# A hybrid decoder step on one core: FFN activations in a ring of single chunks, a pool of its own for the conditioning weights, and the mixer's conditioning moved into the first FFN

## The chip, the cores and the metric

The program runs on one core of one Trainium2 chip. The metric is the device time of one execution in microseconds. Names of engines: PE is TensorE (matmuls; PEld are its weight loads), DVE is VectorE, ACT is ScalarE, POOL is GpSimd, SP is SyncE, which here issues nearly all loads from HBM. Lines such as L302 are lines of the kernel before.

## The reference

One layer over 256 prompt tokens and 32 sample tokens (8 sequences of 4), model width 2048, everything in float32:

```
x += 1/2 * g1 * SwiGLU_1(mod(rms(x); sh1, sc1))          # 2048 -> 5632 -> 2048
x += g2 * W_out[ GDN(h) ++ Retention(h) ],  h = mod(rms(x); sh2, sc2)
x += 1/2 * g3 * SwiGLU_2(mod(rms(x); sh3, sc3))
y  = mod(rms(x); shift, scale)
sh1, sc1, g1, ..., sh3, sc3, g3 = split(silu(c) @ w_ada + b_ada, 9)     # per sequence; 2 more for the end
mod(h; shift, scale) = h * (1 + scale) + shift
```

The gated delta rule (GDN) and the retention are chunked recurrences with 8 heads each. The conditioning `silu(c) @ w_ada` has only nine rows (one prompt, eight samples) but a weight of 2048 columns for each of its 11 segments.

## The kernel before

The 288 tokens lie along the free axis and the channels on the partitions. A dense product is cut into weight blocks of 128 output channels. A block of a 2048-deep product (`wg`, `wu`, `win`, `wout`) is 1 MiB and has 16 chunks of 128 x 128, a block of the down product (`wd`) has 11. SP loads a block into a tile of the pool `raw` (4 tiles); ACT copies it to a rounded high part (`whi`, L295) and DVE forms the low part (`wlo`, L298), both in the pool `hilo`, by halves of 8 chunks. Each chunk is then three matmuls into one PSUM tile `acc`: high by high, high by low, low by high (L302 to L304, `three`). The next block is loaded and its first half split while a block runs (`start`, called at chunk 4 of 16 or at once for `wd`).

Conditioning: a segment of 2048 columns takes 16 tiles of 1 MiB (`raw<-wada`, also in the pool `raw`). `ada_tile` (L211) multiplies one tile, as four 32-column matmuls side by side, into the PSUM tile `pada`; after the sixteenth, ACT copies `pada` to `adas`, PE transposes it and DVE adds the bias (`ada_turn`, `ada_out`). A `Feed` is a list of segments. Its `tick(rate)`, called after every weight block, adds to a debt; whenever the debt reaches `BURST`, so many tiles are loaded and multiplied between two blocks. `one` takes a tile at once, `load` issues a load ahead, `until` finishes segments.

Stages in order: the start, where the first norm and the first 16 gate/up chunks run on pieces of the channels as their conditioning (`wadaq`) arrives, with weights `w1q`; the first FFN (to about 968 us); the mixer (to about 1710 us: projections `win`, then `wout`); the second FFN. In an FFN the 44 activation chunks form four groups of `GK` = 11. The gate/up blocks of group g come before the down product of group g - 1, and the activations (`aH`, `aL`: high and low part) of a group are one tile of 11 chunks in a pool with two buffers. Segments 2, 4, 3 are fed from the start through the first FFN, segments 5, 7, 6 in the mixer, segments 8, 10, 9 in the second FFN; a segment must be there before what uses it (4 and 3 for the mixer's norm, 5 for the residual behind `wout`, 7 and 6 for the third norm).

In the mixer each head's small dependent steps (`gdn_task`, `ret_task`, group tasks) are generators; `side.pump`, called after every chunk of a dense product, puts their next step between the chunks, so that on PE a step stands a fixed number of chunks behind the one before. A scheduler then fixes the order of every engine's instructions, moving an instruction back when its inputs are not ready by its own reckoning; on the chip each engine works through its list in order. `decay_rows` (L855) lets POOL load the decay sums of a head into the tile `z` from a small DRAM tensor `gd`, and DVE's subtraction at L861 waits for it.

```
def norm_to_h(nm, A, B, feed):
    feed.one()
    with tc.issue_after(nm.mm.ins):
        feed.one()
    rb, rs = nm.rows(), None
    with tc.issue_after(nm.mm.ins):
        feed.one()
```

These three single tiles stand where PE waits for a norm: before the last sum of squares, after it, and after the row of 1/rms.

Of the kernel before, what the change touches and what calls it, by code (L numbers as in the profile page):

```python
# [9 lines left out]
F32 = mybir.dt.float32  # L10
# [6 lines left out]
P = 128  # L17
# [91 lines left out]
class Side:  # L109
    """Small dependent steps, traced between the chunks of the dense products."""  # L110
# [26 lines left out]
# in slots of one chunk of a dense product: between a side task's steps, after slow steps, between turns  # L137
# [16 lines left out]
def build(tc, a):  # L154
# [27 lines left out]
    cst = cp.tile([P, CW - P], F32, name="cst")  # L182
# [23 lines left out]
    # conditioning: one segment of 2048 columns, 16 row tiles  # L206
# [8 lines left out]
    def ada_turn(ps, n):  # L215
        s = adar.tile([P, 512], F32, name="adas")
# [6 lines left out]
    def ada_out(out, tp, bs, g):  # L223
        """out [P, n, 9] += bias and, for a scale, (1 + .) * gain; tp [P, j, c, 32], block c * j + j"""
# [9 lines left out]
    class Seg:  # L234
# [3 lines left out]
        def step(self, k, w):  # L238
# [48 lines left out]
    # weight tiles, split into two float32r parts  # L287
# [20 lines left out]

    def start(key):
        """load a weight block and split its first half"""  # L310
# [6 lines left out]
    def block_steps(key, xh, xl, pauses=()):  # L317
# [7 lines left out]
        for k in range(nk):  # L325
# [10 lines left out]
            three(ps, hi[:, o:o + P], lo[:, o:o + P], xh[:, k], xl[:, k], k == 0, k == nk - 1)  # L336
# [23 lines left out]
    class Norm:  # L360
        """Sums of squares over the channels, then a row of 1/rms on all partitions."""
# [52 lines left out]
    def sample_post(t, rs, k0, k1, B, eng=None, out=None):  # L414
        """modulated sample columns of some chunks"""
# [4 lines left out]
    def h_chunks(rb, rs, k0, k1, A, B, pre=None):  # L420
        """channel chunks of the modulated norm, split; the first of them as soon as can be"""
# [27 lines left out]
    def norm_to_h(nm, A, B, feed):  # L449
# [4 lines left out]
        with tc.issue_after(nm.mm.ins):  # L454
            feed.one()
# [12 lines left out]
    class Ffn:  # L468
        def __init__(self, wd, gseg, feed, es):
            self.fp = es.enter_context(tc.tile_pool(name="ffn", bufs=2))  # L470
            self.wd, self.gseg, self.feed = wd, gseg, feed

        def acts(self):
            return (self.fp.tile([P, GK, T], F32R, name="aH"), self.fp.tile([P, GK, T], F32R, name="aL"))

        def act(self, pg, pu, aH, aL, i):
# [5 lines left out]
            split(aH[:, i], aL[:, i], t1)  # L482

        def gate_up(self, n, i0, rate, acts=None, skip=0):
            aH, aL = acts or self.acts()
            for i in range(skip, GK):
# [4 lines left out]
                self.act(pg, pu, aH, aL, i)  # L491
            return aH, aL
# [19 lines left out]
    def groups(f, first, n, off, rates, after, aseg, late=None, second=None):  # L512
        """gate/up of a group goes ahead of the down product of the group before"""
        acts = first
        for g in range(1, NG):
            begun = (second, GQ - GK) if g == 1 and second else ()
            nxt = f.gate_up(n, g * GK - off, rates[0] if g == 1 else rates[1], *begun)
# [4 lines left out]
            f.down(g - 1, *acts, rates[2])  # L522
# [1004 lines left out]
```

## Time and profile before

| | |
|---|---|
| three runs | 2621.33, 2621.54, 2629.79 us (median 2621.54) |
| span of the profiled execution | 2625.5 us (the page gives no other time for it) |
| mean granted TensorE clock | 0.992 |
| PE busy with matmuls | 2556.1 us, 97% |
| DVE, ACT, POOL busy | 1548.6, 973.5, 223.2 us |
| moved by DMA | 579.55 MB, 221 GB/s in the mean |

A busy PE in these views is one that has a matmul in flight. The main matmuls start every 0.13 us though each is shown for about 0.30 us, since they overlap; so the time of a piece of PE work is read as the distance between starts. A number in brackets behind a row of the timeline is the idle time of the engine just before it, with what ended it.

### The profile page before, as it was taken

What the parts mean: (1) busy time and instruction counts of PE and PEld (TensorE: products, weight loads), DVE (VectorE), ACT (ScalarE), POOL (GpSimd) and SP (SyncE); (2) the same over time, 40 slices, a digit from 0 to 9 for tenths busy, and PEclk for the clock granted to TensorE, in tenths of its full rate; (3) what the DMA queues carried; (4) which work ended last, traced back from release to release, by engine and by line L of the source; (5) the groups of instructions that cost most, each with busy time, mean ns of one, the idle gap of its engine ahead of it and who ended that gap; (6) DMA issues with size and microseconds to landing.
All of it is one profiled execution on the core that took longest, in us unless ns stands there. A gap on an engine that the chain in (4) does not pass through costs nothing.

```text
span 2625.5 us, 47975 instructions
## 1 busy us (share of the span) xinstructions
PE 2556.1 (97%) x19579; PEld 2383.3 (91%) x19579; DVE 1548.6 (59%) x3435; ACT 973.5 (37%) x1501; POOL 223.2 (9%) x409
## 2 busy tenths in 40 slices
PE   7999999999999999999999999999999999999997
PEld 6888899999999989888888898989999999999997
DVE  4667645445545577666876787664444544554556
ACT  4233433333333345342333333343333333333334
POOL 0000000000000031111311221210000000000002
PEclk9999999999999999999999999999999999999998
DMA  8776766556655685554656656655565655665553
GB/s 313 282 271 250 289 236 235 214 188 219 232 213 184 243 280 200 183 193 160 255 188 239 220 213 248 219 209 213 221 224 188 245 194 210 208 235 198 200 204 114
DMA packets 97357, 579.55 MB, mean 221 GB/s; under 512 B 11431, under 2 KB 11696, under 8 KB 45808
## 3 DMA queue, kind: packets, MB, share of 16 engines
q1 hardware_dynamic: 91472, 558.60, 58.7%
q0 software_dynamic: 5520, 17.82, 2.1%
q8 instruction: 153, 2.51, 0.4%
q14 instruction: 68, 0.56, 0.1%
q10 hardware_dynamic: 144, 0.07, 0.0%
HBM read 561.94 MB, written 14.50 MB: 220 GB/s over the span
## 4 chain that ended last, share of the span: by engine, by line
PE 88%; DVE 5%; DMA 3%; issue 2%; ACT 1%; POOL 1%; ACTq 0%; SPq 0%; POOLq 0%; DVEq 0%
PE acc L302 26%; PE acc L304 26%; PE acc L303 26%; PE pada L211 5%; PE mp L704 3%; DMA raw<-w1q 1%; DMA z<-gd 1%; DVE wlo L298 1%; ACT whi L295 1%; PE mp L1097 0%; DVE hx L426 0%; DVE hL L431 0%; PE mp L833 0%; POOL or L897 0%; DMA xT<-xT 0%
## 5 line engine op out<-in xcount | busy, mean ns | idle before, releaser
L298 DVE TENSOR_TENSOR wlo<-raw,whi 128x512 fp32r<-128x512 f32 (+1 forms) x1408 | 947.9, 701 | 750.8 <-ACT whi L295 739.8
L295 ACT ACTIVATE whi<-raw 128x1024 fp32r<-128x1024 f32 (+1 forms) x768 | 745.6, 971 | 1363.7 <-PE acc L303 998.4
L302 PE MATMUL acc<-hH,whi 128*128 128x288 f32 x4096 | 1237.4, 303 | 13.4 <-POOL hH L441 4.5
L304 PE MATMUL acc<-hH,wlo 128*128 128x288 f32 x4096 | 1216.0, 297 | 0.1
L303 PE MATMUL acc<-hL,whi 128*128 128x288 f32 x4096 | 1201.4, 294 | 0.9 <-DVE hL L444 0.4
L302 PEld LDWEIGHTS acc<-hH,whi 128*128 128x128 f32 x4096 | 773.6, 189 | 79.6 <-issue 35.4
L303 PEld LDWEIGHTS acc<-hL,whi 128*128 128x128 f32 x4096 | 783.4, 191 | 7.9 <-issue 3.8
L304 PEld LDWEIGHTS acc<-hH,wlo 128*128 128x128 f32 x4096 | 770.9, 188 | 1.4 <-DVE wlo L298 0.8
L302 PE MATMUL acc<-aH,whi 128*128 128x288 f32 x1408 | 415.9, 295 | 0.0
L303 PE MATMUL acc<-aL,whi 128*128 128x288 f32 x1408 | 414.8, 295 | 0.0
L304 PE MATMUL acc<-aH,wlo 128*128 128x288 f32 x1408 | 414.4, 294 | 0.0
L302 PEld LDWEIGHTS acc<-aH,whi 128*128 128x128 f32 x1408 | 264.4, 188 | 15.9 <-ACT whi L295 10.9
L304 PEld LDWEIGHTS acc<-aH,wlo 128*128 128x128 f32 x1408 | 264.4, 188 | 0.0
L303 PEld LDWEIGHTS acc<-aL,whi 128*128 128x128 f32 x1408 | 264.3, 188 | 0.0
L211 PE MATMUL pada<-raw,cS 128*32 128x512 f32 (+2 forms) x1792 | 184.4, 519 | 7.6 <-DMA raw<-wadaq 7.6
L211 PEld LDWEIGHTS pada<-raw,cS 128*32 128x32 f32 x1792 | 49.6, 114 | 68.0 <-issue 59.4
L383 POOL TENSOR_TENSOR ss<-ss,hx 128x288 f32<-128x288 f32 x42 | 36.5, 869 | 871.0 <-ACT hx L377 870.3
L462 DVE SCALAR_TENSOR_TENSOR xT<-acc,ada_G,xT 128x256 f32<-128x256 f32 x128 | 61.9, 484 | 22.3 <-PE acc L304 17.7
L481 DVE TENSOR_TENSOR t<-t,acc 128x288 f32<-128x288 f32 x72 | 32.7, 454 | 69.6 <-PE acc L304 69.6
L506 POOL DMA_DIRECT2D xd<-xT x16 | 9.0, 560 | 563.1 <-DVE xT L465 563.1
L355 ACT ACTIVATE aH<-t 128x288 fp32r<-128x288 f32 x88 | 37.8, 429 | 17.4 <-DVE t L481 17.3
L356 DVE TENSOR_TENSOR aL<-t,aH 128x288 fp32r<-128x288 f32 x88 | 39.7, 451 | 0.7 <-ACT aH L355 0.5
(350 smaller groups left out, 1393.1 us busy)
## 6 DMA issues: line engine op xcount, KB each, us to landing
raw<-wada SPq DMA_DIRECT2D x144, 1024.0 KB, 4.8
raw<-wd SPq DMA_DIRECT2D x128, 704.0 KB, 4.2
raw<-wg SPq DMA_DIRECT2D x72, 1024.0 KB, 4.9
raw<-wu SPq DMA_DIRECT2D x72, 1024.0 KB, 5.0
raw<-win SPq DMA_DIRECT2D x64, 1024.0 KB, 4.9
raw<-wadaq SPq DMA_DIRECT2D x32, 1024.0 KB, 6.1
raw<-w1q SPq DMA_DIRECT2D x64, 512.0 KB, 4.4
raw<-wout SPq DMA_DIRECT2D x16, 1024.0 KB, 5.7
```

Of the source, the lines that this page charges most:

```text
L211: mm = E.matmul(ps[32 * c:32 * c + 32, :n], cS[:, k, :], w[:, n * c:n * c + n], start=(k == 0), stop=(k == NC - 1), skip_group_check=True, ...
L295: S.activation(hi[:, b], src[:, b], AF.Copy)
L298: V.tensor_tensor(lo[:, b], src[:, b], hi[:, b].bitcast(F32), ALU.subtract)
L302: E.matmul(ps[:, :T], h_, xh, start=first, stop=False)
L303: E.matmul(ps[:, :T], h_, xl, start=False, stop=False)
L304: E.matmul(ps[:, :T], l_, xh, start=False, stop=last)
L355: S.activation(hi, x, AF.Copy)
L356: V.tensor_tensor(lo, x, hi.bitcast(F32), ALU.subtract)
L383: G.tensor_tensor(self.ss, self.ss, sq, ALU.add)
L462: V.scalar_tensor_tensor(xT[:, j, :SEQ], ps[:, :SEQ], g[:, j, 0:1], x0[:, :SEQ], ALU.mult, ALU.add)
L481: V.tensor_tensor(t1, t1, pu[:, :T], ALU.mult)
L704: E.matmul(out, lhsT, rhs, start=start, stop=stop, skip_group_check=True)
```

## The change

- The activations are single chunks in a ring of `GK + LEAD` = 20 tiles each for `aH` and `aL`, where they were two tiles of 11 (and, at the start, further ones for partial sums). With that, the gate/up blocks of a group are split: 9 of its 11 chunks go before the down product of the group before, 2 after it.
- Conditioning weights get a pool of their own (`adaw`, 3 tiles) in both FFNs; `raw` is left to the weight blocks there. In the mixer the two tiles that are still loaded ahead lie in `raw`.
- `BURST` is 3 where it was 2. Each `tick` issues one load ahead when fewer than three are under way.
- Segments 5, 7, 6 join the first feed, with higher rates; the `feed.tick` and `feed.until` calls in the mixer are gone. In the first `norm_to_h` three tiles (of segment 8) stand behind the row of 1/rms, where it was one.
- The table `cst` moves from the permanent pool to the mixer's pool and is loaded at the mixer's beginning, by POOL; `adas` shares a tag with `wlo`; the outputs of the conditioning have two buffers each.

```diff
-BURST = 2
+BURST = 3
+LEAD = 9
...
-    cst = cp.tile([P, CW - P], F32, name="cst")
...
-        s = adar.tile([P, 512], F32, name="adas")
+        s = hilo.tile([P, 512], F32, name="adas", tag="wlo")
...
-                out = res[self.seg] = adar.tile([P, NC, 9], F32, name=t, tag=t)
+                out = res[self.seg] = adar.tile([P, NC, 9], F32, name=t, tag=t, bufs=2)
...
+            self.pool = raw
...
-                w = raw.tile([P, D], F32, name="raw")
+                w = self.pool.tile([P, D], F32, name="raw")
...
         def tick(self, rate):
             self.debt += rate
+            if len(self.ahead) < BURST:
+                self.load()
             while self.debt >= BURST:
...
-    def norm_to_h(nm, A, B, feed):
+    def norm_to_h(nm, A, B, feed, more):
...
-            feed.one()
+            for _ in range(more):
+                feed.one()
...
+            feed.pool = es.enter_context(tc.tile_pool(name="adaw", bufs=BURST))
...
-        def acts(self):
-            return (self.fp.tile([P, GK, T], F32R, name="aH"), self.fp.tile([P, GK, T], F32R, name="aL"))
+        def slot(self, name, dt=F32R):
+            return self.fp.tile([P, T], dt, name=name, tag=name[:2], bufs=GK + LEAD)
...
-            split(aH[:, i], aL[:, i], t1)
+            aH.append(self.slot("aH"))
+            aL.append(self.slot("aL"))
+            split(aH[-1], aL[-1], t1)
...
-            nxt = f.gate_up(n, g * GK - off, rates[0] if g == 1 else rates[1], *begun)
+            f.gate_up(n, g * GK - off, rates[0], LEAD, *nxt)
...
-            f.down(g - 1, *acts, rates[2])
+            f.down(g - 1, *acts, rates[1])
+            f.gate_up(n, g * GK - off, rates[0], GK, *nxt)
...
-    feed = Feed([(2, "GQ"), (4, "A", 1), (3, "B")])
+    feed = Feed([(2, "GQ"), (4, "A", 1), (3, "B"), (5, "G"), (7, "A", 2), (6, "B")])
...
-            w = raw.tile([P, D], F32, name="raw")
+            w = feed.pool.tile([P, D], F32, name="raw")
             nc.sync.dma_start(out=w, in_=a["wadaq"][PIECE0[self.n] + self.i])
...
-    feed = Feed([(5, "G"), (7, "A", 2), (6, "B")])
-    nm = groups(ff, acts[0], 1, GQ, (0.45, 0.3, 0.32), feed, 4, late, acts[1])
+    feed2 = Feed([(8, "GQ"), (10, "A", 3), (9, "B")])
+    feed2.pool = feed.pool
+    nm = groups(ff, acts[0], 1, GQ, (0.87, 0.6), feed2, 4, 6, late, acts[1])
+    norm_to_h(nm, res[4], res[3], feed2, 3)
     fs.close()
-    norm_to_h(nm, res[4], res[3], feed)
-    feed2 = Feed([(8, "GQ"), (10, "A", 3), (9, "B")])
+    feed2.pool = raw
     nm = mixer(tc, a, locals())
...
-    first = ff.gate_up(2, 0, 0.4)
-    nm = groups(ff, first, 2, 0, (0.4, 0.3, 0.32), None, 10)
+    ff.gate_up(2, 0, 0.35, GK, *first)
+    nm = groups(ff, first, 2, 0, (0.35, 0.32), None, 10, 3)
...
-    cst = L["cst"]
+    cst = c1.tile([P, CW - P], F32, name="cst")
+    nc.gpsimd.dma_start(out=cst, in_=a["cst"][:, P:])
...
             ps = block("win", 8 * i + h)
-            feed.tick(RATE)
...
-    feed.until(1)
...
-LOADS = (14, 15)
+LOADS = (13, 14, 15)
```

How the order of instructions moves is shown at three places. On SP, at the mixer's beginning, the loads of the kernel before alternate between `win` blocks, conditioning tiles (`wada`) and states of the recurrence (`st<-sg`), and go on with three `win` and two `wada` in turn through the whole mixer:

```order
L314 DMA raw<-win 128x2048
L262 DMA raw<-wada 128x2048
L1078 DMA st_11964<-sg 128x1024
L314 DMA raw<-win 128x2048 x3
L262 DMA raw<-wada 128x2048
L1078 DMA st_11997<-sg 128x1024
L1078 DMA st_12043<-sg 128x1024
L1078 DMA st_12104<-sg 128x1024
L262 DMA raw<-wada 128x2048
L314 DMA raw<-win 128x2048 x3
```

The same place on SP after the change:

```order
L266 DMA raw<-wada 128x2048 x3
L323 DMA raw<-win 128x2048 x3
L266 DMA raw<-wada 128x2048 x2
L323 DMA raw<-win 128x2048
L1085 DMA st_12367<-sg 128x1024
L1085 DMA st_12400<-sg 128x1024
L1085 DMA st_12446<-sg 128x1024
L1085 DMA st_12507<-sg 128x1024
L323 DMA raw<-win 128x2048 x31
```

Five conditioning tiles are loaded around the mixer's beginning, and then none until its last blocks: 31 `win` loads stand in a row.

On PE, also in the mixer, a burst of two tiles (`pada`) stood between two blocks of the kernel before; three chunks of the second block follow, and then a head's transposes (`fv`, L1004):

```order
L304 MATMUL acc_12347<-hH_84,wlo_12349 128x288
L211 MATMUL pada_10294<-raw_12430,cS_94 32x512 x4
L211 MATMUL pada_10294<-raw_12436,cS_94 32x512 x4
L302 MATMUL acc_12459<-hH_84,whi_12376 128x288
L303 MATMUL acc_12459<-hL_85,whi_12376 128x288
```

The same blocks on PE after the change (here `acc_12738` and `acc_12838`), with the transposes again three chunks into the second:

```order
L309 MATMUL acc_12738<-hL_85,whi_12739 128x288
L310 MATMUL acc_12738<-hH_84,wlo_12740 128x288
L308 MATMUL acc_12838<-hH_84,whi_12767 128x288
L309 MATMUL acc_12838<-hL_85,whi_12767 128x288
L310 MATMUL acc_12838<-hH_84,wlo_12768 128x288
```

The burst is gone and the transposes stand behind the same chunks as before, so PE comes to them earlier by the burst.

On SP, at a down product of the first FFN, the kernel before has pairs of conditioning loads between six or seven `wd` loads:

```order
L314 DMA raw<-wu 128x2048
L262 DMA raw<-wada 128x2048 x2
L314 DMA raw<-wd 128x1408 x7
L262 DMA raw<-wada 128x2048 x2
L314 DMA raw<-wd 128x1408 x6
```

After the change, at a down product of the first FFN:

```order
L323 DMA raw<-wu 128x2048
L323 DMA raw<-wd 128x1408
L266 DMA raw<-wada 128x2048 x3
L323 DMA raw<-wd 128x1408 x4
L266 DMA raw<-wada 128x2048 x3
```

Three conditioning loads now stand in a row between four `wd` loads.

## Rows read from the trace of the kernel before

**Rows 1.** The page's first part: engine, busy us, share of the span, instructions.
```profile
PE 2556.1 (97%) x19579; PEld 2383.3 (91%) x19579; DVE 1548.6 (59%) x3435; ACT 973.5 (37%) x1501; POOL 223.2 (9%) x409
```

**Rows 2.** Windows: stretch, length, busy of PE, PEld, DVE, ACT, POOL; clock, DMA share, GB/s.
```profile
10.00:20.00 10.00, 5.12 (x78) 4.82 (x82) 4.95 (x14) 3.70 (x11) 0.87 (x1) 1.00 1.01 422
300.00:968.00 668.00, 667.91 (x5063) 637.29 (x5062) 353.12 (x697) 242.17 (x312) 22.69 (x36) 1.00 0.62 222
990.00:1640.00 650.00, 628.06 (x4782) 566.06 (x4781) 468.77 (x1278) 246.72 (x524) 137.16 (x253) 0.99 0.58 209
```

**Rows 3.** PE's timeline around a burst of two tiles: start, us, engine, line, names.
```profile
1991.09 0.29 PE L304 MATMUL acc<-hH,wlo 128*128 128x288 f32 x1
1991.31 1.92 PE L211 MATMUL pada<-raw,cS 128*32 128x512 f32 x16
1993.17 0.40 PE L302 MATMUL acc<-hH,whi 128*128 128x288 f32 x1
```

**Rows 4.** PE's timeline around a single tile.
```profile
2536.84 0.29 PE L304 MATMUL acc<-aH,wlo 128*128 128x288 f32 x1
2537.07 1.06 PE L211 MATMUL pada<-raw,cS 128*32 128x512 f32 x8
2538.06 0.40 PE L302 MATMUL acc<-aH,whi 128*128 128x288 f32 x1
```

**Rows 5.** Windows of pada's instructions alone: PE, PEld, ACT, clock, DMA share, GB/s.
```profile
977.00:1640.00 663.00, 48.17 (x360) 9.53 (x360) 1.80 (x3) 0.99 0.58 212
```

**Rows 6.** PE's timeline at the mixer's norm.
```profile
973.58 1.07 PE L211 MATMUL pada<-raw,cS 128*32 128x512 f32 x8
976.28 0.29 PE L721 MATMUL acc<-hH,whi 128*32 128x288 f32 x1 [1.64 <-DVE hs L418]
```

**Rows 7.** PE's waits from 20 to 300 us: total, times, longest.
```profile
PE acc L302 <- ACT whi L295: 1.7, 3, 1.1
...
PE pada L211 <- DMA raw<-wadaq: 1.3, 2, 0.7
```

**Rows 8.** The chain of waits from 262 to 282 us: start, us, what.
```profile
263.77 3.24 DMA raw<-w1q
...
268.42 8.23 DMA raw<-w1q
```

**Rows 9.** PE's timeline in the mixer: two bursts and the waits behind them.
```profile
1143.98 1.92 PE L211 MATMUL pada<-raw,cS 128*32 128x512 f32 x16
...
1151.15 0.48 PE L1004 MATMUL mp<-ident,fv 128*128 128x128 f32 x1 [2.51 <-DVE bv L1005]
...
1385.17 1.93 PE L211 MATMUL pada<-raw,cS 128*32 128x512 f32 x16
...
1394.52 0.30 PE L989 MATMUL mp<-ident,fq 128*128 128x128 f32 x1 [2.99 <-DVE fq L941]
```

**Rows 10.** PE's waits from 990 to 1650 us: total, times, longest.
```profile
PE mp L704 <- ACT vn L1034: 3.0, 2, 1.6
```

**Rows 11.** DVE's waits from 1000 to 1640 us: total, times, longest.
```profile
DVE d L861 <- DMA z<-gd: 20.7, 6, 4.8
```

**Rows 12.** The tile z: its DMAs' time to landing.
```profile
DMA to landing us min/median/max: 3.4/6.2/7.6
```

**Rows 13.** DMA issues from 1383 to 1392 us: KB each, median us to landing.
```profile
raw<-win SPq DMA_DIRECT2D x2, 1024.0 KB, 9.1
raw<-wada SPq DMA_DIRECT2D x1, 1024.0 KB, 12.1
...
z<-gd POOLq DMA_DIRECT2D x1, 128.0 KB, 7.6
```

**Rows 14.** Window behind the wait at 1148 us; columns as in Rows 2.
```profile
1151.00:1154.40 3.40, 3.25 (x15) 3.23 (x15) 1.95 (x8) 1.39 (x3) 0.28 (x2) 0.50 0.88 371
```

**Rows 15.** DMA issues of the whole span: KB each, median us to landing.
```profile
raw<-wada SPq DMA_DIRECT2D x144, 1024.0 KB, 4.8
...
cst<-cst POOLq DMA_DIRECT2D x1, 1211.0 KB, 8.4
```

More of the change, by code (lines that the diff above doesn't have):

```diff
@@ L307, in build, with chunk @@
     pre = {}
+    def chunk(x, k):
+        return x[k] if isinstance(x, list) else x[:, k]
     def start(key):
@@ L335, in block_steps @@
             o = k % 8 * P
-            three(ps, hi[:, o:o + P], lo[:, o:o + P], xh[:, k], xl[:, k], k == 0, k == nk - 1)
+            three(ps, hi[:, o:o + P], lo[:, o:o + P], chunk(xh, k), chunk(xl, k), k == 0, k == nk - 1)
         return ps
@@ L481, in act, with gate_up @@
             V.tensor_tensor(t1, t1, pu[:, :T], ALU.mult)
-            split(aH[:, i], aL[:, i], t1)
-        def gate_up(self, n, i0, rate, acts=None, skip=0):
-            aH, aL = acts or self.acts()
-            for i in range(skip, GK):
+            aH.append(self.slot("aH"))
+            aL.append(self.slot("aL"))
+            split(aH[-1], aL[-1], t1)
+        def gate_up(self, n, i0, rate, i1, aH, aL):
+            for i in range(len(aH), i1):
                 pg = block(f"wg{n}", i0 + i)
@@ L510, in down, with groups @@
                         nm.later.append(put)
-    def groups(f, first, n, off, rates, after, aseg, late=None, second=None):
-        acts = first
+    def groups(f, acts, n, off, rates, after, aseg, nseg, late=None, second=None):
         for g in range(1, NG):
-            begun = (second, GQ - GK) if g == 1 and second else ()
-            nxt = f.gate_up(n, g * GK - off, rates[0] if g == 1 else rates[1], *begun)
+            nxt = second if g == 1 and second else ([], [])
+            f.gate_up(n, g * GK - off, rates[0], LEAD, *nxt)
             if g == 1:
@@ L521, in groups @@
                     late()
-            f.down(g - 1, *acts, rates[2])
+            f.down(g - 1, *acts, rates[1])
+            f.gate_up(n, g * GK - off, rates[0], GK, *nxt)
             acts = nxt
         nm = Norm()
-        f.down(NG - 1, *acts, rates[2], nm, after, aseg, off > 0)
-        f.feed.until(3)
+        f.down(NG - 1, *acts, rates[1], nm, after, aseg, off > 0)
+        f.feed.until(nseg)
         return nm
     fs = ExitStack()
-    feed = Feed([(2, "GQ"), (4, "A", 1), (3, "B")])
+    feed = Feed([(2, "GQ"), (4, "A", 1), (3, "B"), (5, "G"), (7, "A", 2), (6, "B")])
     ff = Ffn("wd1", 2, feed, fs)
-    A1 = adar.tile([P, NC, 9], F32, name="ada_A", tag="ada_A")
-    B1 = adar.tile([P, NC, 9], F32, name="ada_B", tag="ada_B")
+    A1 = adar.tile([P, NC, 9], F32, name="ada_A", tag="ada_A", bufs=2)
+    B1 = adar.tile([P, NC, 9], F32, name="ada_B", tag="ada_B", bufs=2)
     class Piece:
@@ L586, in build @@
     rB = ff.fp.tile([P, T], F32, name="rB", bufs=1)
-    part = [(ff.fp.tile([P, GK, T], F32, name=n), ff.fp.tile([P, GQ - GK, T], F32, name=f"{n}q", bufs=1))
-            for n in ("aH", "aL")]
-    part = [[x[:, i] for x, n in ((t, GK), (u, GQ - GK)) for i in range(n)] for t, u in part]
+    part = [[ff.slot(n, F32) for _ in range(GQ)] for n in ("aHq", "aLq")]
     off = 0
-    acts = []
+    acts = [([], []), ([], [])]
     for n, (k0, k1) in enumerate(PIECES):
@@ L617, in build @@
                 if last:
-                    if i in (0, GK):
-                        acts.append(ff.acts())
-                    ff.act(part[0][i], part[1][i], *acts[i // GK], i % GK)
+                    ff.act(part[0][i], part[1][i], *acts[i // GK])
             if not last:
@@ L675, in mixer @@
     pv, bc, mp, acc, xT, hH, hL = (L[k] for k in ("pv", "bc", "mp", "acc", "xT", "hH", "hL"))
-    ident, ones1, mhalf, feed, res = (L[k] for k in ("ident", "ones1", "mhalf", "feed", "res"))
+    ident, ones1, mhalf, res = (L[k] for k in ("ident", "ones1", "mhalf", "res"))
     block, split, residual, side, b4 = (L[k] for k in ("block", "split", "residual", "side", "b4"))
@@ L976, in gdn_head @@
         ps = block("win", 24 + h)
-        feed.tick(RATE)
         gate(ps, f["z"], gt["z"][:, cs])
@@ L1412, in ffn @@
     def ffn(n, g0, off):
-        gu = lambda g: [(f"w{w}{n}", i, NC) for i in range(max(0, g * GK - off), (g + 1) * GK - off) for w in "gu"]
+        gu = lambda g, i0, i1: [(f"w{w}{n}", i, NC) for i in range(max(0, g * GK - off + i0), g * GK - off + i1) for w in "gu"]
         dn = lambda g: [(f"wd{n}", g * NC + j, GK) for j in range(NC)]
-        r = gu(0) if g0 == 0 else []
+        r = gu(0, 0, GK) if g0 == 0 else []
         for g in range(1, NG):
-            r += gu(g) + dn(g - 1)
+            r += gu(g, 0, LEAD) + dn(g - 1) + gu(g, LEAD, GK)
         return r + dn(NG - 1)
```

22 lines of the change are left out of this document (6 added, 16 removed).

## Prediction

> **What bounds the kernel now.** I read the page's first part, then busy time by stage, then PE's and DVE's waits where PE is not full, then the timeline around single bursts. PE has a matmul in flight for 2556.1 of 2625.5 us [rows 1]. In the first FFN it lacks 0.1 us of 668 (667.91), while DMA moves 222 GB/s; the reader is to see that nothing there waits for a load. In the mixer it lacks 21.9 us of 650 (650 - 628.06) [rows 2]. So a change gains where it takes work from PE or shortens the mixer's waits; a load that comes earlier in an FFN gains nothing. The profiled span is 2625.5 us; the runs lie at 2621.33 to 2629.79 with a median of 2621.54. I make the sum against the span and take it off the median.
>
> **Longer bursts.** A burst of two tiles puts 1993.17 - 1991.09 = 2.08 us between two starts of PE that are otherwise 0.13 apart: 1.95 us [rows 3]. A single tile makes 2538.06 - 2536.84 = 1.22, so 1.09 us [rows 4]. A further tile thus costs 0.86 us and the visit itself 0.23 us. Three tiles, which no row shows, should cost 1.95 + 0.86 = 2.81; the bounds are 1.95 + 1.09 (nothing saved) and 1.95 + 0.73 (another 0.13 saved). The order of instructions has 86 visits for the 144 `wada` tiles before and 64 after: 22 x 0.23 = 5.1 us off, with bounds 0 and 8. The tiles themselves are as many as before.
>
> **Two more tiles at the mixer's norm.** PE idles 1.64 us there after its third single tile [rows 6]. The change puts five tiles in place of three. But its fourth and fifth need the places of the first two, so their loads start late, and in PE's order they stand behind 12 and 29 matmuls of the next product, whose chunks of h arrive no faster than DVE makes them. They fill part of that slack: two tiles that elsewhere cost 2 x 0.86 are worth between 0 and 1.7 us, and I take 1.0 off.
>
> **The start.** From 20 to 300 us PE waits 1.3 us for `wadaq` and 1.7 us for ACT's `whi` [rows 7]; behind the latter stand loads of `w1q` that take 3.24 and 8.23 us of the chain, just after a burst [rows 8], because bursts and weights share four tiles. With three tiles more both have their places ahead. The waits can go wholly (3.0 off) or stay; the stretch from 10 to 20 us, where DMA is full (share 1.01) [rows 2], does not change. I take 2.0 off.
>
> **The mixer's conditioning goes to the first FFN.** 45 tiles (360 records of 8 to a tile) leave the mixer [rows 5], about 22 visits of 1.95 us = 43 us, and cost the same in the first FFN, where PE has no idle time to hide them. What decides is how much of the 43 us PE really gains in the mixer. There the bursts stood between a product and the side steps that wait for DVE or ACT, and gave these time. Two places show it: 7.2 us after a burst starts PE waits 2.51 us for the transposes of `fv`, and 9.4 us after another it waits 2.99 us for `fq` [rows 9]. With the burst gone, PE comes to them earlier and waits 1.95 us longer unless DVE is quicker too. Two waits for ACT's `vn`, 3.0 us together [rows 10], follow a burst as closely. Four such places: 4 x 1.95 = 7.8 us on. Steps that now arrive just in time would add to this; all 22 visits would be 43 us.
>
> Against it: DVE works in order, and in this stretch it stands 20.7 us in six waits for the DMA of `z` [rows 11], which lands after 3.4 to 7.6 us, in the median 6.2 [rows 12]. In the case behind the 2.99 us, two `win` blocks and a conditioning tile were issued within the same few us and took 9.1 and 12.1 us, and `z` 7.6 [rows 13]. After the change the mixer loads only `win`, one block as each of four places comes free, so `z` should land nearer its 3.4. If half of the 2.8 us between median and minimum comes off at four places, that is 4 x 1.4 = 5.6 off. The Trainium skill, DMA: Bandwidth & Descriptors, Issuing engines are not separate DMA queues, says that loads of all issuing engines run on the same 16 DMA engines and interleave; rows 13 agree (7.6 us beside full queues, against 3.4 at best), and by that rule alone most of the 2.8 us would come off, which is the rival on the faster side below. I take 7.8 - 5.6 = 2 us on for the mixer; its bounds are 17 off (all but 5 of the 21.9 us) and 43 on.
>
> **Edits at nothing.** Three conditioning loads in a row ahead of a weight block in the first FFN: the stage moved 222 GB/s x 668 us = 148 MB; with 48 more tiles (50 MB) in 668 + 45 us it needs 278 GB/s, and 422 were reached from 10 to 20 us [rows 2]. The cover is the ring of four `raw` tiles, now for weights alone; without it see the rival. The split gate/up: chunk 10's activation is read 30 matmuls (3.9 us) into the first down block, and only the last group lacks other blocks between; 0, at most 1 us at each of two places. `cst` is issued by POOL before the norm's power and lands after 8.4 us [rows 15]; its first reader stands 88 matmuls (11.6 us) behind the norm; 0, at most 2. `adas` takes a place of `wlo` once a segment, so that DVE's next split starts up to four chunks later and still ends within the block; 0, at most 0.5 us in 9 segments.
>
> **Sum.** -5.1 - 1.0 - 2.0 + 2 = -6.1 us: 2619.4 on the span, 2615.4 on the median. Forecast 2615.5 us, with 2606 to 2626 as its own range.
>
> **Rivals.**
>
> *z lands at its best (faster).* If every `z` takes 3.4 us, DVE's 20.7 us shrink to 20.7 - 6 x 2.8 = 3.9, and the PE waits that hang on it go in spite of the lost cover: about 15 of the 21.9 us, and with them a stretch of half clock. After the 2.51 us wait the granted clock was 0.50 for 3.4 us [rows 14], which is 1.2 in place of 2.4 GHz and costs 1.7 us. That gives -8.1 - 15 - 1.7 = -25: 2597 us. For it: the crowded queue at just these places. Against it: 18 of the 22 bursts had no named wait behind them that a faster `z` could remove, and the best of nine landings need not become the rule.
>
> *The lost cover comes back as waits (slower).* PE in the mixer reaches its side steps 1.95 us early at most of the 22 places, and DVE, busy 468.77 of 650 us [rows 2] and soon of some 607, does not follow. It decides the sign from 22 / 1.95 = 11 places on (8.1 + 13 us to be more than 0.5% slower); at 13 places it is 25 us: 2621.5 - 8.1 + 25 = 2638. For it: side steps follow each other by fixed numbers of chunks. Against it: only four places wait now, and the scheduler has put the transposes of `fq` 14 to 20 matmuls further back where the burst went. The Trainium skill, TensorE: Matmul & The Clock Gate, The HAM clock gate, says that the array's clock falls to half after idling; rows 14 agree (0.50 after a 2.51 us wait), and by it every second such wait would cost 1.7 us more.
>
> *Weights come late in the first FFN (slower).* Two `win` blocks issued together took 9.1 us, 4.55 each [rows 13]; at that pace three tiles and a `wd` block take 13.7 + 3.1 = 16.8 us, and three `wd` blocks of PE work only 3 x 33 x 0.132 = 13.1. 3.7 us at each of 64 x 0.6 / 3 = 13 visits is 47; half of it gives 2639 us. For it: SP's order has the three in a row. Against it: a single tile landed in 4.8 us with others beside it [rows 15], pairs with fewer free places cost no wait in the stage before, and 422 GB/s needs 9 us for the same bytes.
>
> *The order does not do what it says:* the third tile's load waits for a place and splits the bursts. Then the visits stay at 86 and -5.1 falls away: 2620.5 us, no change. A place comes free 25 us before it is needed, so I give it little.
>
> **Chances.** Forecast 0.53, z at its best 0.22, lost cover 0.12, late weights 0.08, split bursts 0.05. A change of 0.5%, 13 us, is about what a measurement of this kernel can tell from none; faster than that means below 2608.4, slower above 2634.6. Faster: 0.22 and 0.05 of the forecast's own spread, 0.27. Slower: 0.11 of lost cover and 0.05 of late weights, together 0.16. The same: 0.57. The range 2596 to 2638 leaves out the half of the fast rival beyond its centre and most of the slow cases' upper part, 0.2 together.
>
> **What would show it.** Right: visits of three tiles with 2.94 us between the neighbouring starts; PE still full from 300 us to the end of the first FFN, which ends some 43 us later, and a mixer shorter by about 41; `z` landing in 4 to 5 us; no `w1q` in the chain at 260 to 290 us. Wrong: a mixer shorter by under 25 us (lost cover) or by over 50 (z); PE waiting for `whi` or `wlo` in the first FFN, with `wd` loads that land after 10 us and more.

## The result and the profile after

The changed kernel takes 2604.47 us in the median (2602.56 to 2604.69), the kernel before 2623.78 beside it: ratio 0.9916, 95% interval 0.9901 to 0.9931. The forecast of 2615.5 had the sign and a third of the size. The result lies inside the prediction's range of 2596 to 2638, but below the forecast's own (2606 to 2626), on the faster side, to which the prediction gave 0.27. A repeat gave 2602.98 against 2627.86, ratio 0.9904 [0.9890, 0.9919]. The profiled spans are 2625.5 and 2602.6 us, 22.9 apart. A span is 1.8 us shorter than the measured time of the same execution (2604.39 us for the one profiled after, 0.1 below its median); by this the execution profiled before took about 2627.3 us (an estimate, its time is not on record), 3.5 above its median, so some 3.6 us of the 22.9 are this execution's.

The page's first part after the change, where PE's busy time falls by 13.7 us against [rows 1]:

```profile
PE 2542.4 (98%) x19579; PEld 2378.5 (91%) x19579; DVE 1541.1 (59%) x3435; ACT 974.0 (37%) x1501; POOL 217.7 (8%) x408
```

The first FFN and the mixer of [rows 2] after the change, moved to where they now lie (columns as there):

```profile
300.00:1004.00 704.00, 704.00 (x5362) 640.77 (x5361) 348.47 (x701) 238.76 (x310) 22.31 (x34) 1.00 0.73 275
1026.00:1640.00 614.00, 593.25 (x4539) 568.45 (x4538) 476.04 (x1290) 251.97 (x531) 137.29 (x262) 1.00 0.43 154
```

The first FFN carries 275 GB/s and PE lacks nothing of 704 us; the mixer carries 154 and PE still lacks 20.75 us (614.00 - 593.25), where it lacked 21.9. So the transfers moved and PE's idle time stayed.

Whole stages show the rest. They begin with the first dense matmul of the start, of the first FFN, of the mixer and of the second FFN. The mixer's window alone begins later, behind the matmuls that stand among the pieces of its norm: 6.2 us after the first FFN's end before, 8.8 after the change, which now hold two conditioning tiles. Before:

```profile
24.60:229.00 204.40, 195.51 (x1679) 171.61 (x1679) 118.38 (x241) 71.24 (x99) 8.35 (x19) 0.98 0.78 279
229.00:976.30 747.30, 743.25 (x5615) 701.70 (x5616) 415.32 (x837) 276.64 (x368) 27.83 (x47) 1.00 0.64 228
982.50:1716.40 733.90, 709.58 (x5390) 643.11 (x5388) 526.16 (x1388) 279.83 (x569) 158.58 (x288) 1.00 0.58 210
1716.40:2608.40 892.00, 889.39 (x6708) 850.93 (x6709) 466.58 (x907) 326.51 (x422) 17.96 (x27) 1.00 0.57 206
```

After:

```profile
24.50:221.60 197.10, 192.53 (x1689) 169.34 (x1689) 118.34 (x239) 71.16 (x99) 8.73 (x19) 0.99 0.83 296
221.60:1012.60 791.00, 788.59 (x6000) 714.69 (x6001) 415.60 (x852) 279.25 (x371) 27.91 (x46) 1.00 0.74 279
1021.40:1700.60 679.20, 656.23 (x5017) 628.35 (x5016) 516.67 (x1369) 275.89 (x562) 152.60 (x288) 1.00 0.45 158
1700.60:2585.40 884.80, 883.98 (x6667) 850.64 (x6668) 465.70 (x907) 327.05 (x422) 17.94 (x27) 1.00 0.56 202
```

Length less busy is PE's idle time: 8.9, 4.1, 24.3 and 2.6 us before, 4.6, 2.4, 23.0 and 0.8 after. That is 9.1 us less, 4.3 of it at the start. Over the whole span it is 69.4 and 60.2 us, 9.2 less, so the parts that these windows leave out have no share in it.

The granted clock is the second source. Before, it stood at 0.50 or 0.51 in these stretches (1.2 in place of 2.4 GHz):

```profile
24.60:28.00 3.40, 3.37 (x25) 2.65 (x26) 2.45 (x6) 1.06 (x1) 0.00 (x0) 0.50 0.78 261
99.70:106.50 6.80, 5.07 (x20) 4.98 (x21) 6.14 (x12) 3.82 (x6) 1.97 (x5) 0.50 0.83 288
229.40:232.80 3.40, 3.40 (x16) 3.27 (x15) 2.85 (x6) 0.51 (x1) 0.18 (x1) 0.50 0.36 147
976.90:980.30 3.40, 3.23 (x14) 2.75 (x15) 3.40 (x10) 1.42 (x3) 3.18 (x9) 0.50 1.02 419
1219.20:1222.60 3.40, 3.40 (x16) 1.98 (x16) 2.19 (x7) 0.00 (x0) 0.84 (x2) 0.51 0.27 34
1717.60:1721.00 3.40, 3.28 (x14) 2.96 (x14) 3.40 (x10) 1.85 (x5) 2.64 (x6) 0.50 1.01 424
```

With [rows 14] that is 27.2 us. The program's last 13.6 us before and 14.7 after are at half clock as well; PE does next to nothing there (1.49 us in both), and they are left out. After the change there are two stretches:

```profile
24.50:27.90 3.40, 3.38 (x25) 2.66 (x26) 2.87 (x7) 1.06 (x1) 0.00 (x0) 0.50 1.03 414
1014.40:1017.80 3.40, 3.40 (x16) 1.33 (x16) 3.40 (x9) 1.97 (x6) 2.11 (x5) 0.50 1.00 419
```

In the repeat the first of them was absent and its start took 195.70 us in place of 197.10, with the same instructions and the same idle time (4.6 us): by this pair of executions one such stretch costs 1.4 us. The other stood behind the norm again.

```profile
24.00:219.70 195.70, 191.12 (x1690) 168.22 (x1690) 118.42 (x239) 71.30 (x99) 8.73 (x19) 1.00 0.83 300
```

Third, the visits. A visit is an unbroken run of conditioning matmuls on PE. From the first dense matmul on the conditioning has 117 visits before and 93 after (parts of a burst that a side step cuts count apart). A burst of three answers to [rows 3]:

```profile
611.20 0.29 PE L310 MATMUL acc<-aH,wlo 128*128 128x288 f32 x1
611.42 2.78 PE L212 MATMUL pada<-raw,cS 128*32 128x512 f32 x24
614.14 0.40 PE L308 MATMUL acc<-aH,whi 128*128 128x288 f32 x1
```

614.14 - 611.20 = 2.94 us, as forecast. Together: idle -9.1, clock -(27.2 - 6.8) / 3.4 x 1.4 = -8.4, visits -24 x 0.23 = -5.5, in all -23.0 of the 22.9 seen. The idle time and the number of visits are read; the price of a visit is that of whole bursts, and the clock's part is the price of one stretch times six. PE's busy time fell by 13.7, and clock and visits make 13.9 of it.

DVE's wait for `z` in 1034 to 1650 us, against [rows 11], and its landing, against [rows 12]:

```profile
DVE d L870 <- DMA z<-gd: 10.3, 4, 3.2
```
```profile
DMA to landing us min/median/max: 3.4/4.8/8.1
```

Half of DVE's wait is gone. PE's idle time in the mixer hardly moved, yet it was cut differently: the waits of 2.51 and 2.99 us of [rows 9] are gone, and the longest named one is 1.9 us. PE's waits from 1026 to 1700 us:

```profile
PE mp L1076 <- DVE on L907: 5.9, 6, 1.7
PE mp L831 <- DVE Tn L1032: 2.9, 5, 0.7
PE mp L1350 <- DVE on L920: 2.3, 2, 1.2
PE mp L1319 <- DVE on L920: 1.9, 1, 1.9
PE mp L1011 <- DVE bv L1012: 1.3, 3, 0.4
```

### The profile page after: what moved, and what is told of

Same layout as the page of the kernel before. It is cut to its first block, busy times and chain, and to the rows that moved or that the text cites. A ratio compares the mean times of both kernels' runs of the same rounds, so it can differ in the third digit from the quotient of the medians.

```text
span 2602.6 us, 47978 instructions
## 1 busy us (share of the span) xinstructions
PE 2542.4 (98%) x19579; PEld 2378.5 (91%) x19579; DVE 1541.1 (59%) x3435; ACT 974.0 (37%) x1501; POOL 217.7 (8%) x408
## 3 DMA queue, kind: packets, MB, share of 16 engines
q8 instruction: 153, 2.51, 0.4%
## 4 chain that ended last, share of the span: by engine, by line
PE 90%; DVE 5%; POOL 2%; issue 1%; ACT 1%; DMA 1%; SPq 0%; ACTq 0%; POOLq 0%; DVEq 0%
PE acc L308 27%; PE acc L309 26%; PE acc L310 26%; PE pada L212 6%; PE mp L713 2%; DVE wlo L304 1%; PE mp L1104 0%; DMA z<-gd 0%; PE mp L842 0%; POOL rv L918 0%; ACT whi L301 0%; POOL or L906 0%; ACT kd L882 0%; ACT y L673 0%; DMA xT<-xT 0%
## 5 line engine op out<-in xcount | busy, mean ns | idle before, releaser
L308 PE MATMUL acc<-hH,whi 128*128 128x288 f32 x4096 | 1222.2, 299 | 8.3 <-POOL hH L450 4.0
L309 PEld LDWEIGHTS acc<-hL,whi 128*128 128x128 f32 x4096 | 771.0, 188 | 6.4 <-issue 2.1
L308 PEld LDWEIGHTS acc<-aH,whi 128*128 128x128 f32 x1408 | 263.9, 187 | 16.8 <-issue 15.9
L212 PE MATMUL pada<-raw,cS 128*32 128x512 f32 (+2 forms) x1792 | 178.8, 520 | 6.5 <-DMA raw<-wadaq 6.4
L627 DVE TENSOR_TENSOR aLq<-acc,aLq 128x288 f32<-128x288 f32 x64 | 29.1, 455 | 26.6 <-PE acc L310 26.2
```

The costliest lines, as they stand in the source:

```text
L212: mm = E.matmul(ps[32 * c:32 * c + 32, :n], cS[:, k, :], w[:, n * c:n * c + n], start=(k == 0), stop=(k == NC - 1), skip_group_check=True, ...
L308: E.matmul(ps[:, :T], h_, xh, start=first, stop=False)
L309: E.matmul(ps[:, :T], h_, xl, start=False, stop=False)
L627: V.tensor_tensor(dst, ps[:, :T], dst, ALU.add)
```

## The experiments

Ratios are to the kernel before, run on the same chip in the same rounds; intervals are 95%. The changed kernel's own is 0.9916, and 0.9904 in the repeat. A profile shows one execution, and its span is compared with the 2602.6 us of the changed kernel's.

**Bursts of two in the changed kernel.**

```diff
-BURST = 3
+BURST = 2
...
-            feed.pool = es.enter_context(tc.tile_pool(name="adaw", bufs=BURST))
+            feed.pool = es.enter_context(tc.tile_pool(name="adaw", bufs=3))
```

> The changed kernel with bursts of two tiles in place of three; the pool of three tiles stays. If a visit of PE to the conditioning costs 0.23 us whatever its length, 22 more visits cost 5.1 us: 2609.6 us against the changed kernel's 2604.5, and 2.08 us between the starts around each pair. If a longer burst saves nothing (each tile 0.98 us), 2604.5. If the loads of three in a row cost waits in the first FFN, it is faster: below 2602.

Measured 2611.55 us, 0.9947 [0.9933, 0.9961]; span 2607.9, 5.3 above the changed kernel's. There are 107 visits in place of 93, 14 more and not the 22 expected: 14 x 0.23 = 3.2. A further 1.8 us is idle time in the first FFN (one wait of 3.4 us for a `wada` tile; with `BURST` at 2, `tick` also keeps only two loads ahead, though the pool has three places). Together that is 5.0 of the 5.3, so the price of a visit holds. By the medians the difference is 7.1 us; the profiled execution is 1.8 us faster than its median.

**The mixer's conditioning back in the mixer,** in twos through `raw`. The rates of the FFNs follow, and one tile stands behind the row of 1/rms of the mixer's norm; all else is as changed.

```diff
-    feed = Feed([(2, "GQ"), (4, "A", 1), (3, "B"), (5, "G"), (7, "A", 2), (6, "B")])
+    feed = Feed([(2, "GQ"), (4, "A", 1), (3, "B")])
...
+    feed1 = Feed([(5, "G"), (7, "A", 2), (6, "B")])
+    feed1.burst = 2
...
+            L["feed1"].tick(RATE)
```

> The changed kernel with segments 5, 7 and 6 given back to the mixer, in pairs through the pool raw as in the kernel before; ring, own pool in the FFNs, bursts of three there and the start stay. Theory (the move gains by the granted clock and little else): the mixer's idle time of PE stays at 23 to 25 us, some half-clock stretches come back in it, and some 9 more visits cost 2 us: 2604.5 + 2 + 3.4 + 1 = 2611 us. Rival one (z lands late again and PE waits for it): idle time of the mixer 30 us and more, 2616 or above. Rival two (the move only lost cover): PE's idle time in the mixer falls by 8 us and more and the kernel is faster than 2602.

Measured 2613.16 us, 0.9949 [0.9935, 0.9963]; span 2610.3. Two rows of PE's timeline in the mixer, each with the wait ahead of it:

```profile
1138.82 0.48 PE L1016 MATMUL mp<-ident,fv 128*128 128x128 f32 x1 [2.48 <-DVE bv L1017]
```
```profile
1380.31 0.30 PE L1001 MATMUL mp<-ident,fq 128*128 128x128 f32 x1 [3.38 <-DVE fq L953]
```

The two long waits are back, and at each the clock fell (columns as in [rows 2]):

```profile
1138.20:1141.60 3.40, 2.78 (x12) 2.77 (x13) 2.42 (x9) 1.38 (x4) 0.28 (x2) 0.50 0.99 417
1380.50:1383.90 3.40, 3.40 (x18) 3.40 (x17) 2.71 (x9) 2.77 (x14) 0.72 (x3) 0.51 0.94 389
```

Idle time in the mixer is 24.0 us against 23.0. By this run, 7.7 us longer in its span, the move is worth its visits (108 against 93, 3.5 us) and the mixer's clock (6.8 us of half clock against none, 2.8), little else. This agrees with both the forecast (two effects that cancel) and a theory that neither exists; the two runs with one side cut, below, tell them apart.

**The move alone,** made to the kernel before, with the second buffers for the conditioning's outputs and the place of `adas` that go with it.

```diff
-    feed = Feed([(2, "GQ"), (4, "A", 1), (3, "B")])
+    feed = Feed([(2, "GQ"), (4, "A", 1), (3, "B"), (5, "G"), (7, "A", 2), (6, "B")])
...
-    nm = groups(ff, acts[0], 1, GQ, (0.45, 0.3, 0.32), feed, 4, late, acts[1])
+    nm = groups(ff, acts[0], 1, GQ, (0.9, 0.68, 0.68), feed2, 4, late, acts[1])
...
-            feed.tick(RATE)
```

> The kernel before, with one part of the change alone: the segments 5, 7 and 6 are multiplied in FFN1, at twice its rate of conditioning, and the mixer holds none; tiles still come in twos through the shared pool, and the activations keep their ring. Theory (the move saves switches into the conditioning's matmuls only where bursts grow, and half clock in the mixer; TensorE's waits in the mixer do not come from the conditioning): switches stay at about 115, so nothing there; half clock in the mixer 6.8 us to 0, worth 3.4; idle time of the mixer stays at 23 to 25 us; about 2621 against the before of the same chip (ratio 0.998), down to 2616 if a stretch of half clock goes at the start by chance. Rival, loads out of the mixer are worth its z waits: 2626 - 10 = 2616 with idle at 14 to 18 us. Rival, lost cover: idle at 30 us or more and no gain. Rival, FFN1's shared pool can't feed twice the rate: FFN1's idle time rises from 4 to over 10 us.

Measured 2639.34 us, 1.0063 [1.0050, 1.0077]: 0.6% slower. The mixer does as expected (idle 24.0, no half clock); the visits are 107, not the 115 expected. The first FFN's waits decide. The longest of PE's from 300 to 1750 us:

```profile
PE pada L211 <- DMA raw<-wada: 10.0, 5, 4.8
```

The two long ones, 8.8 us together, stand at 1018 to 1033 us, where the last two tiles of the six segments are loaded only as they are multiplied, and beside them the clock stood at half for 17.1 us. The first FFN took 815.0 us, against 798.2 in the changed kernel with twos: 9.5 us more idle and 14.9 us more at half clock (6.1 us at 1.4 a stretch, 7.5 if half of the time is lost) make nearly all of these 16.8. The rival of the shared pool has its sign, 13.7 us of idle time in the first FFN against 4.1 before. In this form, with these rates, the move costs more than it brings. In the changed kernel these tiles are loaded ahead into a pool of their own; that this, and not a higher rate, is what makes the move pay is argued and not shown.

**The start's loads back in `raw`,** in the changed kernel.

```diff
-            w = feed.pool.tile([P, D], F32, name="raw")
+            w = raw.tile([P, D], F32, name="raw")
```

> The changed kernel with the start's conditioning tiles (wadaq) back in the pool raw, which they then share with the start's weights as in the kernel before; all else stays. Theory (the start's 7 us come from the own pool: waits of 3 us for loads, and the half-clock stretch of 6.8 us at 100 us that they bring on): the 1152nd main matmul starts at 229 us again and not at 221.6, 2612 us. Rival (the start gained by its order or by chance of the clock): 2604.5 us, with the stretch at 100 us still away.

Measured 2612.16 us, 0.9942 [0.9928, 0.9957]. Its start, with one stretch of half clock as in the profile after:

```profile
24.80:227.00 202.20, 193.94 (x1689) 169.30 (x1689) 116.83 (x239) 71.78 (x99) 8.57 (x19) 0.99 0.82 289
```

202.20 against 197.10: by this profile the pool is worth 5.1 us at the start, 3.7 of it idle time (8.3 against 4.6). The stretch of half clock at 100 us did not come back in it. But the profiled execution (2608.22 us, granted clock 0.997) is the fastest of five; the other four have 0.994 or 0.995 and up to 2613.50 us, and the median is 7.7 us above the changed kernel's. What these lost, and whether that stretch is part of it, no profile shows.

**The mixer's cover cut, its loads kept,** in the kernel before. Here cover means the time that a burst gives the other engines before PE's next side step; the kernel leaves out most of the product that fills it.

```diff
-            ada_tile(self.ps, k, w, 512)
+            ada_tile(self.ps, k, w, 16 if sliver and k else 512)
```

> The kernel before, with the mixer's conditioning loads and bursts kept, but each conditioning matmul of the mixer behind a segment's first tile covers 16 columns in place of 512 (most of that product is left out). So the transfers of the mixer stay, and nearly all of the work that could cover TensorE's waits goes: 45 tiles of about 0.98 us less some 0.2 that remain, 35 us. Theory (waits of the mixer are not covered by the conditioning): idle time of TensorE in the mixer stays at 24 us, VectorE's waits for z at about 20 us, the mixer falls from 734 to about 699, in all about 2590. Rival, lost cover: idle rises by 8 us or more to over 32, in all about 2598 or above. Rival, the transfers set the waits: with the bursts shorter the loads press the z transfers more and idle rises together with the z waits.

Measured 2599.35 us, 0.9900 [0.9887, 0.9914].

**The mixer's loads cut, its cover kept,** in the kernel before.

```diff
-            if s < len(self.q):
+            if s < len(self.q) and self.still:
+                self.ahead.append(hH.rearrange("p k t -> p (k t)")[:, :D].bitcast(F32))
+            elif s < len(self.q):
```

> The kernel before, with the mixer's conditioning bursts kept on TensorE but fed from a resident tile, so that their 48 loads of 1 MB are left out (these segments hold wrong values). The complement of the kernel with short matmuls: cover stays, transfers go. Theory (the z transfers are waited for by VectorE and not passed on to TensorE): VectorE's waits for z fall from 20 to about 10 us, idle time of TensorE in the mixer stays at 23 to 25 us, the mixer at 730 to 734, about 2624 (ratio 0.9985 to 1.0). Rival, faster z transfers are worth what VectorE no longer waits for: idle 14 to 18, the mixer at 724 to 728, about 2617.

Measured 2622.74 us, 0.9982 [0.9972, 0.9991]. The kernel leaves out 45 loads (99 of `wada` in place of 144), since the norm's three stand ahead of the mixer. The mixer with the cover cut, and below it with the loads cut:

```profile
981.10:1686.90 705.80, 676.19 (x5389) 639.32 (x5387) 519.37 (x1389) 278.90 (x568) 153.16 (x288) 1.00 0.60 219
```
```profile
979.40:1705.70 726.30, 707.96 (x5383) 642.08 (x5382) 525.19 (x1385) 278.78 (x566) 158.74 (x288) 1.00 0.42 147
```

Idle time is 29.6 us with the cover cut and 18.3 with the loads cut, against 24.3: 5.3 up and 6.0 down. Profiles that differ only outside the mixer have 22.9 to 24.6 there, so both are more than their spread. DVE's waits for `z`, 1000 to 1640 us, in the one and the other, against [rows 11]:

```profile
DVE d L865 <- DMA z<-gd: 16.9, 5, 4.7
```
```profile
DVE d L865 <- DMA z<-gd: 14.4, 6, 3.1
```

The rival by which shorter bursts let the loads press `z` harder falls: with the cover cut the waits for `z` are shorter, not longer. The theory of these two runs, that neither effect exists, fell by the idle time, which is one profile each: the bursts did cover waits, and the loads did make some. The time of the second run alone would not tell. Its median is only 3.8 us below the 2626.51 of the kernel before, near the theory's 2624, and the profiled execution (2616.42) is the fastest of eleven. The granted clock goes with this spread: it is 0.995 in the five executions of up to 2619.97 us and 0.993 or 0.994 in the six from 2622.74 on.

**One tile, not three, behind the row of 1/rms at the mixer's norm.**

```diff
-    norm_to_h(nm, res[4], res[3], feed2, 3)
+    norm_to_h(nm, res[4], res[3], feed2, 1)
```

> The changed kernel with one tile in place of three behind the row of the mixer's norm. Theory: the two tiles fill slack of PE that is there anyway and cost 2 x 0.86 us where they go instead: 2604.5 + 1 to 1.7 = 2606 us. Rival: they only push the mixer's first products back by their own length: 2604.5, no change. The half-clock stretch behind the norm stays in both.

Measured 2605.8 us, 0.9922 [0.9907, 0.9937]; span 2603.2, 0.6 above. That profile had one more stretch of half clock (at 1698.9 us, 1.4 us); without it, it would be 0.8 us faster than the changed kernel's. By the medians it is 1.3 us slower, as the theory has it. Even the sign is open: inconclusive.

**Bursts of four, five chunks ahead.**

```diff
-BURST = 3
+BURST = 4
...
-LEAD = 9
+LEAD = 5
```

> The changed kernel with bursts of four tiles and loads held five ahead in place of three tiles and nine ahead. Theory (each switch into and out of the conditioning's matmuls costs 0.23 us, bursts hold nothing up): switches fall from 93 to about 78, so 3.5 us less, about 2603 against 2606 for the changed kernel on this chip (ratio 0.991). Rival, longer bursts hold up the engines that wait for FFN1's tiles: FFN1's idle time rises from 2.4 to 6 us or more, and nothing is gained. Rival, five ahead is too few beside bursts of four: TensorE waits for a conditioning weight at some bursts, 2 to 4 us each, 2610 or more.

Measured 2606.9 us, 0.9928 [0.9914, 0.9941]. There are 74 visits, but in the first FFN PE waits for tiles:

```profile
PE pada L212 <- DMA raw<-wada: 6.4, 5, 2.1
```

From 288 us on, among these waits, 10.2 us are at half clock. There `f.feed.until(1)` stands behind the first `LEAD` chunks; with five, the first segment is not yet done and its last tiles are multiplied as they land.

**Bursts of four, seven chunks ahead** (`LEAD = 7`), and the changed kernel again beside it.

> The changed kernel with bursts of four tiles and seven activation chunks ahead of a down product in place of three and nine. Theory (each visit costs 0.23 us; what the kernel with four tiles and five chunks ahead lost, 5.5 us of idle time and 10.2 us of half clock, came at one place, where the first segment had to be finished after ten blocks and its last tiles were multiplied as they landed; with seven ahead 12 of its 16 tiles are done by then and the other 4 are loaded): visits about 75 against 93, FFN1's idle time back at 2 to 3 us and no half clock in it, 4 us less than the changed kernel: about 2600 (ratio 0.990 to this chip's before). Rival, four loads in a row press the weights behind them: FFN1's idle time stays at 6 us or more, 2605 or above.

> The changed kernel itself, on the same chip and in the same rounds as the kernel with bursts of four and seven ahead, for a direct comparison: 2604 to 2606 (ratio 0.9916 to this chip's before). What its profile shows again is taken as its own: visits 93, idle time of the mixer 22 to 25 us, no half clock in the mixer. Theory that half clock outside the mixer falls by chance: its stretches at the start or behind the norm stand elsewhere than in the first profile. Rival, they are a fixed property: the same two, at 24 and 1014 us.

Measured 2599.42 us (2598.55 to 2600.08), 0.9890 [0.9873, 0.9906], against 2602.98 (2602.17 to 2603.67) on the same chip: 3.6 us less, and the two ranges do not meet. Its burst of four:

```profile
656.51 0.29 PE L310 MATMUL acc<-hH,wlo 128*128 128x288 f32 x1
656.74 3.64 PE L212 MATMUL pada<-raw,cS 128*32 128x512 f32 x32
660.31 0.40 PE L308 MATMUL acc<-hH,whi 128*128 128x288 f32 x1
```

3.80 us between starts is 2.94 + 0.86 again. There are 74 visits, 19 fewer than 93: -4.4 us. The first FFN idles 3.6 us, 1.2 more than in the changed kernel and above the 2 to 3 expected; 2.8 of them are one wait for a tile at the norm, at the place where the changed kernel waits 1.63 us for DVE. -4.4 + 1.2 is -3.2 of the -3.6. This version beats both kernels.

## Why the prediction was right in sign and small in size

The span fell by 22.9 us where the forecast had 6.1. The 16.8 us between them are, nearly, 8.4 of the clock, 4.0 of the start, 3.3 of the mixer's idle time, 1.8 of the second FFN's and 0.4 of the visits, less the 1.0 forecast for the norm.

**Longer bursts (-5.1): the price right, the number partly by luck.** The trace has 2.94 us for three tiles, 3.80 for four, and 24 visits fewer: -5.5. But about 10 of the 24 come with the move and not from the length of a burst: with bursts of two there are 107 visits in place of 117, in the changed kernel as with the move alone. In the mixer before, side steps cut bursts (33 visits for 48 tiles), in the first FFN hardly (27 for 50). The longer bursts have 14 visits, -3.2.

**Two more tiles at the norm (-1.0): not shown.** Two rows of PE's timeline at the norm after the change, which answer to [rows 6]:

```profile
1012.62 0.29 PE L730 MATMUL acc<-hH,whi 128*32 128x288 f32 x1 [1.63 <-DVE hs L427]
...
1015.63 1.93 PE L212 MATMUL pada<-raw,cS 128*32 128x512 f32 x8
```

The wait for DVE is as long as before and the fourth tile comes behind 12 matmuls, as the forecast said. But it runs at half clock, 1.93 us for a single tile that takes 1.07 in [rows 6], and the run with one tile does not tell what the two are worth.

**The start (-2.0, bounds -3 to 0): a step that failed.** The term was mis-sized: from the start to 300 us PE's idle time fell by 6.0 us (4.3 in the start, 1.7 in the first FFN), and the start as a whole by 7.3. The forecast counted only the waits that name `wadaq` and `whi`, 1.3 and 1.7 us in [rows 7]. Both went wholly; the second was the first FFN's 1.7. PE's waits from 20 to 230 us after the change:

```profile
PE acc L308 <- POOL hH L450: 4.0, 3, 1.6
PE acc L308 <- DVE hH L450: 2.3, 1, 2.3
PE mp L221 <- ACT adas L218: 0.5, 1, 0.5
```

Before, the same view had, beside the wait for `wadaq` of [rows 7], a longer one for `adas` and two more, for `aHq` and `aH`:

```profile
PE acc L302 <- POOL hH L441: 4.5, 4, 1.8
PE acc L302 <- DVE hH L441: 2.3, 1, 2.3
PE mp L220 <- ACT adas L217: 1.4, 1, 1.4
...
PE acc L302 <- ACT aHq L614: 0.8, 1, 0.8
PE acc L302 <- DVE aH L616: 0.6, 1, 0.6
```

With the tiles in `raw` again, the 3.7 us of idle time that come back stand under four names: 1.6 more for `adas` (2.1 in all), 1.3 for `whi`, 0.6 more for POOL's `hH`, and 0.2 for `wadaq` itself. So the late tile is waited for mostly under the names of what stands behind it, which the forecast did not count. The waits for `aHq` and `aH` did not come back; no run shows what took them off. The pool is worth 5.1 us by that run. Against before, idle time (-4.3) and 6.8 us of half clock (two stretches of 1.4, -2.8) make -7.1 of the start's -7.3.

**The clock: left out of the sum, the larger failed step.** The forecast put it at nothing without a reason and priced it only in rivals, at 1.7 us a stretch where the runs show 1.4. Across the program it made about 8 of the 23 us. In the mixer it goes with the move: 3.4 or 6.8 us at half clock in each of the four profiles with the conditioning there, none in the eight with it in the first FFN. Outside the mixer the stretches stand elsewhere from one execution to the next, so no single stretch there can be put down to a part of the change. The gain as a whole is not the two profiles' accident: the 33 executions of the kernel before beside the experiments have a mean granted clock of 0.990 to 0.995, the eight of the changed kernel 0.996 or 0.997; the profiled ones have 0.992 and 0.996. The Trainium skill, TensorE: Matmul & The Clock Gate, The HAM clock gate, says that the array falls to half clock after idling; the runs agree (2.48 and 3.38 us of waiting, with 0.50 and 0.51 beside them). By that rule alone the 2.99 us wait of [rows 9] would have had its price too; no half clock stood behind it. That every second such wait would cost something, as the lost-cover rival has it, rests on these two waits of [rows 9] alone, of which one was followed by half clock.

**The mixer (+2 = +7.8 - 5.6): both effects are there, their places were wrong.** Cutting the cover alone added 5.3 us of idle time, cutting the loads alone took 6.0 off, and the move of both left 1.3 less, where the forecast had 2 more. That 5.3 is near 7.8 is luck, since none of the four places counted for the cover grew: with the cover cut the waits for `fq` and `bv` shrank (3.0 and 3.8 us to 0.9 and 1.2), and the two for `vn` of [rows 10] stayed:

```profile
PE mp L708 <- ACT vn L1038: 2.9, 2, 1.6
```

These two are gone with the loads cut, so they were the loads' and not the cover's. The added idle time stands elsewhere, at `Tn` (0.3 us to 2.3) and `St` (none to 2.9). The mixer became 54.7 us shorter (52.1 with the stretch at its norm) where the prediction's last part gave 41 and read over 50 as a sign of `z`. That test was badly set. The 45 tiles (38.7 us) left with 30 visits in place of 22 (6.9), since side steps cut bursts, with 2.8 us of clock and 1.3 of idle time; some 5 us remain, among them three segments' transposes, which left too and which neither side of the sum had. In the first FFN, 43.7 us longer, tiles and transposes came back with only 12 visits more.

**The second FFN: not in the sum.** Its idle time fell by 1.8 us; a wait for ACT's `hH` at its beginning went from 1.8 to 0.3. The gain is there too with the conditioning back in the mixer (0.4 us idle in that stage) and is missing with the move alone (2.6), so it is not the move's. No run shows which other part it is.

**The rivals.** `z` at its best did not happen (4.8 us in the median, idle 20.75 of 614). Lost cover is real, but 5.3 us where the rival had 25. Late weights: the landing of a `wada` tile went from 4.8 [rows 15] to 7.8 us, but it is 7.3 with bursts of two and 6.8 with the move alone, so the third load in a row is a small part of that. `wd` blocks took 4.2, as before, and PE waited for none from 300 to 1004 us. The rows of the page after:

```profile
raw<-wada SPq DMA_DIRECT2D x144, 1024.0 KB, 7.8
raw<-wd SPq DMA_DIRECT2D x128, 704.0 KB, 4.2
```

With the move alone, without the new pool, PE waited in the first FFN from 300 us on for conditioning tiles and for no weights. The bursts were not split: from the first FFN on PE has 63 visits, where the order of instructions had 64.

**Open:** which wait sets off each half-clock stretch outside the mixer, and what of the start's clock is the pool's; the one profile with the loads in `raw` had a single stretch there, as after the change, and was the fastest of its five executions.

## What to carry to other kernels

Where the busiest engine is full in one stage and waits in the next, moving work between them is worth only what the second stage really loses; cut the work and its loads one at a time before believing that nothing happens, since two effects of 5 to 6 us can cancel. A wait for a late load shows up under the names of what follows it, so price a starved stage by length less busy time, not by the rows that name the load. When a quota must be met at a fixed place, check how many of its tiles are loaded by then: that decided two of the runs here.

## What the runs showed that was not expected

In these traces half clock did not follow every long wait and did follow short ones: before, 2.99 us of waiting left the clock alone, and two waits of 1.14 and 1.18 us, 1.6 us apart, were followed by 3.4 us at 0.51. The rows ahead of the stretch at 1219 us, before:

```profile
1216.52 0.30 PE L1311 MATMUL mp<-ident,on 128*128 128x128 f32 x1 [1.14 <-DVE skq L1104]
1218.13 1.07 PE L1097 MATMUL mp<-st,kqG 128*32 128x512 f32 x8 [1.18 <-DVE skq L1104]
```

A `wada` tile that landed three us later cost nothing here while three lay ahead, and the 422 GB/s of [rows 2] were not needed: 275 sufficed for a first FFN with twice the conditioning.
